# A 64-byte offset for the split weights of 256-column matmuls, and a new order at three places of the even mixer

## Chip, cores and metric

The kernel runs on one core of one Trainium2 chip. The metric is the device time of one execution in microseconds (us), as a median over runs; lower is better. The profiler also takes one execution apart, instruction by instruction; the rows below are from that one.

## The reference

Two layers over 256 latent tokens and 256 context tokens of width 1024. Each layer is: half-step SwiGLU feed-forward, token mixer, half-step SwiGLU feed-forward, each with an RMSNorm that is scaled and shifted by a modulation (made from `c` and `c_ctx`) and a gated residual. Layer 0 mixes with differential attention and a bidirectional mLSTM, layer 1 with gated linear attention; in layer 1 the context stream stops after the mixer's keys and values.

```python
for l in range(DEPTH):
    mx = (s_lat @ ada_w[l] + ada_b[l]).reshape(bsz, N_MOD, 1, d)
    x = x + 0.5 * mx[:, 2] * swiglu(ada_norm(x, norm_g[l, 0], mx[:, 0], mx[:, 1]), ffn_w_in[l, 0], ffn_w_out[l, 0])
    hctx = hctx + 0.5 * mc[2] * swiglu(ada_norm(hctx, ...), ffn_w_in[l, 0], ffn_w_out[l, 0])
    hx = ada_norm(x, norm_g[l, 1], mx[:, 3], mx[:, 4])
    hc = ada_norm(hctx, norm_g[l, 1], mc[3], mc[4])
    yx, yc = even_mixer(...) if l % 2 == 0 else odd_mixer(...)
    x = x + mx[:, 5] * yx
    x = x + 0.5 * mx[:, 8] * swiglu(...)
return rms_norm(x, final_g)
```

## The kernel before

Everything is kept with features on the 128 partitions and tokens on the columns: 8 tiles `xT` of 128x512 (columns 0 to 255 context, `CTX`; 256 to 511 latent, `LAT`). A product in float32 is made of three fp32r matmuls (lines 147 to 150): each operand is split into a high and a low part (`hh`/`hl` or `gh`/`gl` for the activations, `whi`/`wlo` for the weights), and high by high, high by low and low by high are added in PSUM. Each matmul has its own weight load of 128 columns.

Weights come in 1 MB loads (`load`, line 114, on SP's queue) and are split, a tile of 128x1024 at a time, by ScalarE (cast, line 122) and VectorE (subtraction, line 123) into `whi` and `wlo`, two buffers each. Activations `hh`, `hl` are the moving operand with 512 columns (both streams) or 256 (one stream: `CTX` or `LAT`); in `proj_rows` (line 624, the value projections) it is the other way round, the activations are the stationary operand and `whi`, `wlo` move with 256 columns. Where both streams start a stage (`gemm_first`, line 237), the context's columns go first while the latent's norm is still being made; the weights of two of the four tiles there are kept in `wspare`, tiles of the stage's own pool (`split_spare`, line 134).

Where things lie in a partition follows from the order and the size of the tiles in the code, each rounded up to 32 bytes. The pools stand one behind the other: consts (with `unit_e`, 768 bytes, `xT`, `hh`, `hl` of 2048 bytes each), weights (`raw` of 8192, `whi` and `wlo` of 4096), temps, then the pools of the stage. All of these sizes are multiples of 128 from `xT` to `wlo`, except some small ones between `hl` and `raw` that add up to one; so `hh`, `hl`, `gh`, `gl`, `whi` and `wlo` all start at the same place of 128 bytes (64). Two groups stand apart by 64 bytes: `LAST = slice(T - 16, TT - 16)` (line 32) puts the latent activations of the odd mixer's output projection and of the last feed-forward 16 columns (64 bytes) lower, and in the even mixer's pool the two 4-byte tiles `gb` and `gd` (32 bytes each, rounded) push every tile behind them, `wspare` among them, by 64.

The order on each engine is made by a scheduler from the order of the code, the dependences and its own costs; pools with few buffers set when a bank or tile can be taken again. In the even mixer (line 684): `proj_first` makes the mLSTM's q and k, then the gates' product `psg` (24 matmuls, line 752), then the gates' chain on VectorE and ScalarE (lines 763 to 785), four transposes `pmt` of its result (line 788), then head after head, with the value projections (`rows_pair`) and others in between as the scheduler places them. `psg` is in one of the two `mm` banks that `ps_v` and `ps_fm` also use, until line 778 has read it. The two `stack` calls (lines 1013 and 1015) split q and k of the heads for the scores on ScalarE and VectorE. At the mixer's end (lines 1052 to 1063) the last four output tiles are made, `CTX` first, then `LAT` in the order of tiles 2, 3, 0, 1; between the latent tiles the context's norm (one step of factors, eight of `modulate`) is issued in pieces of 0:2, 2:4, 4:6 and the rest. The latent's squares are summed on GpSimd, except those of features 6 and 7, on VectorE (line 260).

Of the kernel before, what the change touches and what calls it, by code (L numbers as in the profile page):

```python
# [17 lines left out]
P = 128  # L18
D = 1024
KC = D // P  # L20
NS = 3
T = 256
# [14 lines left out]
def backbone_kernel(  # L37
# [43 lines left out]
    unit_e = cp.tile([P, 6, 32], F32, name="unit_e")  # L81
    nc.gpsimd.memset(unit_e, 0.0)
    for i in range(6):
        nc.gpsimd.memset(unit_e[:, i, i : i + 1], 1.0)
# [22 lines left out]

    def table(name):
        tc.keep_in_program_order(nc.scalar.preload_act_table_set(name))
# [15 lines left out]
    def split(r3):  # L125
# [3 lines left out]
        hi3 = hi[:, : a * b].rearrange("p (a b) -> p a b", a=a)  # L129
        lo3 = lo[:, : a * b].rearrange("p (a b) -> p a b", a=a)  # L130
        split_into(hi3, lo3, r3)
        return hi3, lo3
# [11 lines left out]
    def half(r3, m):  # L144
        return split(r3[:, :, m * P : m * P + P])
# [39 lines left out]
    def ada_finish(n, acc, pool, ap):  # L185
# [5 lines left out]
        for j in range(4):  # L191
            for i in range(2):
                nc.tensor.matmul(  # L193
                    ps[32 * j : 32 * j + 32, :256],
                    lhsT=unit_e[:, 2 * (n - first) + i],
# [56 lines left out]
    def stat(k, i, sl, apart=False):  # L252
# [43 lines left out]
    def residual(k, ps, gate, i, sl, nxt):  # L296
        residual_at(k, ps[:, sl], gate, i, sl, nxt)

    def residual_at(k, o, gate, i, sl, nxt):
# [3 lines left out]
        stat(k, i, sl, nxt == (1, 2))  # L303

    def out_pass(pairs, streams, units, acts, bank, gate, nxt, between=()):
# [7 lines left out]
        def fetch(mp, k0, nk, ld, m):  # L313
            if m == 0:
                cur["raw"] = ld(mp)
            return half(cur["raw"], m)
# [40 lines left out]
    def ffn_in(l, f, sl, gh, gl, bank, fp, step, j0=0, spare=None, at=None):  # L357
        w_in = ffn_w_in[l, f]
        for j1 in range(j0, NJ, 2):
            js = range(j1, min(j1 + 2, NJ))  # L360
            r = [load(rows(w_in, c0 + j1 * P, len(js) * P)) for c0 in (0, DFF)]
            if spare and j1 == 0:
                ps = [[bank("ps_ab") for _ in range(2)] for _ in js]
                gemm_first(
                    [(ps[0][a], lambda a=a: half(r[a], 0)) for a in range(2)]
# [237 lines left out]
    def proj_fm(w, c0, n, emit, sl=BOTH):  # L603
        for mp in range(n // 2):
            r3 = load(rows(w, c0 + mp * 256, 256))
            for m in range(2):
                wt = half(r3, m)
# [4 lines left out]
    def proj_first(w, c0, emits, bank, sbank, spare):  # L612
# [4 lines left out]
            [(ps[m], lambda m=m: half(r[0], m)) for m in range(2)]  # L617
# [6 lines left out]
    def proj_rows(w, c0, dst, col):  # L624

        r3 = load(rows(w, c0, 256))
        ps = [mm_bank("ps_v") for _ in range(2)]
        for i in range(2):
            wh, wl = split(r3[:, 4 * i : 4 * i + 4])
            for t in range(4):  # L630
                o = ps[t // 2][:, (t % 2) * T : (t % 2) * T + T]
                for k4 in range(4):
# [30 lines left out]
    def out_weights(w, m0, spares):  # L663
# [3 lines left out]
            half(r[t // 2], t % 2) if sp is None else split_spare(r[t // 2], t % 2, sp) for t, sp in enumerate(spares)  # L667
# [16 lines left out]
    def even_mixer(nxt):  # L684
# [54 lines left out]
        graw = mp_.tile([P, KC, 16], F32, name="graw")  # L739
# [11 lines left out]
        psg = mm_bank("psg")  # L751
# [7 lines left out]
        oneh = mp_.tile([P, H2], F32R, name="oneh")  # L759
        for r in (slice(0, H2), slice(H2, P)):  # L760
            nc.vector.tensor_copy(oneh[r], ident[r, r])
# [17 lines left out]
        nc.scalar.copy(gah, ga)  # L779
# [5 lines left out]
        nc.vector.tensor_tensor(mst[H2:P], mst[0:H2], bcum[0:H2], ALU.add)  # L785
        pmt = bank_m("pmt")
        for t in range(4):
            nc.tensor.transpose(pmt[:, t * P : t * P + P], mst[:, t * P : t * P + P], ident)
# [7 lines left out]
        def rows_pair(c0, dst):  # L796
            for i in range(2):
                proj_rows(w_in, c0 + i * T, dst, i * T)
# [5 lines left out]
        def decay_exps(h):  # L804
            E = {}
            for d in range(2):
                pA = bank_m("pA")
                sel = oneh[:, 32 * d + h : 32 * d + h + 1].to_broadcast([P, P])
# [205 lines left out]
        mlstm_head(0, lambda: rows_pair(2048, mv))  # L1014
        mstk.append(stack(mq[1], mq[3], halves2("wTa4", 1) + slots1(("mq0", 1), ("mq2", 1), ("rsa", 1), ("qk3", 1)), (nc.scalar.copy, nc.scalar.copy, nc.scalar.copy, nc.vector, nc.vector)))
# [440 lines left out]
```

## Time and profile before

| what | us |
|---|---|
| median of 3 runs (1784.91 to 1788.17) | 1787.75 |
| the profiled execution's own time | 1790.07 |
| its span, from the first to the last instruction | 1788.4 |
| TensorE busy in the span | 1748.8 (98%) |
| weight loads busy | 1505.4 (84%) |
| VectorE busy | 1151.9 (64%) |
| ScalarE busy | 742.8 (42%) |
| GpSimd busy | 106.7 (6%) |

The profiled execution took 2.3 us more than the median. A matmul's row gives its start and a modelled duration in which it overlaps the next; the pace of a run of matmuls is read from their starts or their number in a stretch, not from the durations.

### The profile page before, as it was taken

How to read it: one execution, taken by the hardware profiler on the slowest of the kernel's cores; microseconds unless marked ns; L12 is line 12 of the kernel's file. 1: busy time of each engine (PE TensorE's matmuls, PEld its weight loads, DVE VectorE, ACT ScalarE, POOL GpSimd, SP SyncE). 2: the span in 40 equal slices, each digit the busy share in tenths (PEclk: the TensorE clock that was granted, in tenths of full speed). 3: DMA queues.
4: the chain of work that ended last, by engine and by line, in shares of the span. 5: the costliest groups of instructions: out<-in, count | busy, mean ns of one | idle time of the engine just before them, and what ended most of it. 6: DMA issues, size and time to landing. Idle time of an engine off the chain costs nothing.

```text
span 1788.4 us, 24901 instructions
## 1 busy us (share of the span) xinstructions
PE 1748.8 (98%) x10087; PEld 1505.4 (84%) x10087; DVE 1151.9 (64%) x1678; ACT 742.8 (42%) x1286; POOL 106.7 (6%) x172
## 2 busy tenths in 40 slices
PE   7999999999999999999999999999999999999998
PEld 5788888899887798888888898888888998889996
DVE  4677776657668866777753485777533737855555
ACT  3422222247558854222222252222322645654443
POOL 1000000003011111000000010000000200010000
PEclk9999999999999999999999999999999999999999
DMA  9555555544121214455543344555442632236553
GB/s 288 189 166 187 188 165 188 171 130 126 48 71 48 95 48 141 165 187 187 188 149 96 126 146 165 188 189 188 143 149 85 190 118 72 80 109 198 187 195 118
DMA packets 209303, 262.30 MB, mean 147 GB/s; under 512 B 6863, under 2 KB 188662, under 8 KB 209188
## 3 DMA queue, kind: packets, MB, share of 16 engines
q1 hardware_dynamic: 208160, 259.28, 44.4%
q8 instruction: 79, 1.29, 0.3%
q0 software_dynamic: 576, 0.84, 0.2%
q10 hardware_dynamic: 452, 0.59, 0.1%
q14 instruction: 36, 0.29, 0.0%
HBM read 259.64 MB, written 1.05 MB: 146 GB/s over the span
## 4 chain that ended last, share of the span: by engine, by line
PE 84%; DVE 8%; ACT 4%; issue 2%; DMA 2%; POOL 0%; SPq 0%; ACTq 0%; POOLq 0%; DVEq 0%
PE ps_ab L148 15%; PE ps_ab L149 15%; PE ps_ab L150 15%; PE ps_y L148 7%; PE ps_y L150 7%; PE ps_y L149 7%; PE ps_fm L150 2%; PE ps_fm L149 2%; PE ps_fm L148 2%; DVE wlo L123 2%; PE po L911 1%; ACT whi L122 1%; PE ada_ps L193 1%; PE ps_l L1386 1%; PE ps_l L1387 1%
## 5 line engine op out<-in xcount | busy, mean ns | idle before, releaser
L122 ACT CAST whi<-raw 128x1024 fp32r<-128x1024 f32 (+1 forms) x326 | 336.3, 1032 | 824.3 <-PE ps_ab L149 451.2
L123 DVE TENSOR_TENSOR wlo<-raw,whi 128x1024 fp32r<-128x1024 f32 (+1 forms) x326 | 392.5, 1204 | 305.9 <-ACT whi L122 301.3
L149 PE MATMUL ps_ab<-hl,whi 128*128 128x512 f32 (+1 forms) x1360 | 483.6, 356 | 2.6 <-POOL hl L279 2.3
L148 PE MATMUL ps_ab<-hh,whi 128*128 128x512 f32 (+1 forms) x1360 | 484.4, 357 | 1.7 <-ACT whi L122 1.0
L150 PE MATMUL ps_ab<-hh,wlo 128*128 128x512 f32 (+1 forms) x1360 | 482.5, 355 | 1.2 <-DVE wlo L123 1.1
L181 DVE SCALAR_TENSOR_TENSOR acc<-raw_ada,cs,acc 128x1024 f32<-128x1024 f32 x224 | 276.5, 1280 | 48.2 <-DMA raw_ada<-in_ada_w_dram 48.1
L148 PEld LDWEIGHTS ps_ab<-hh,whi 128*128 128x128 f32 x1360 | 255.1, 188 | 44.3 <-ACT whi L122 6.6
L149 PEld LDWEIGHTS ps_ab<-hl,whi 128*128 128x128 f32 x1360 | 255.5, 188 | 39.8 <-POOL hl L279 2.9
L150 PEld LDWEIGHTS ps_ab<-hh,wlo 128*128 128x128 f32 x1360 | 255.4, 188 | 38.7 <-DVE wlo L123 1.8
L150 PE MATMUL ps_y<-gh,wlo 128*128 128x512 f32 (+1 forms) x660 | 229.9, 348 | 0.4
L148 PE MATMUL ps_y<-gh,whi 128*128 128x512 f32 (+1 forms) x660 | 230.0, 348 | 0.0
L149 PE MATMUL ps_y<-gl,whi 128*128 128x512 f32 (+1 forms) x660 | 228.8, 347 | 0.0
L150 PEld LDWEIGHTS ps_y<-gh,wlo 128*128 128x128 f32 x660 | 124.9, 189 | 17.6 <-DVE wlo L123 1.5
L148 PEld LDWEIGHTS ps_y<-gh,whi 128*128 128x128 f32 x660 | 124.9, 189 | 17.0 <-ACT whi L122 1.2
L149 PEld LDWEIGHTS ps_y<-gl,whi 128*128 128x128 f32 x660 | 124.9, 189 | 15.5
L353 DVE TENSOR_TENSOR s<-ps_ab,s 128x512 f32<-128x512 f32 (+1 forms) x88 | 54.7, 622 | 118.0 <-PE ps_ab L150 117.9
L260 POOL TENSOR_TENSOR ssum<-ssum,sq 128x256 f32<-128x256 f32 x25 | 26.2, 1049 | 1103.0 <-ACT sq L258 834.4
L148 PE MATMUL ps_fm<-hh,whi 128*128 128x256 f32 (+1 forms) x256 | 83.9, 328 | 0.0
L150 PE MATMUL ps_fm<-hh,wlo 128*128 128x256 f32 (+1 forms) x256 | 83.5, 326 | 0.0
L149 PE MATMUL ps_fm<-hl,whi 128*128 128x256 f32 (+1 forms) x256 | 83.1, 325 | 0.0
L636 PE MATMUL ps_v<-whi,hh 128*128 128x256 f32 x256 | 74.2, 290 | 1.2 <-ACT mv L640 1.2
L637 PE MATMUL ps_v<-wlo,hh 128*128 128x256 f32 x256 | 74.6, 291 | 0.0
(375 smaller groups left out, 2396.3 us busy)
## 6 DMA issues: line engine op xcount, KB each, us to landing
raw<-in_ffn_w_in_dram SPq DMA_DIRECT2D x84, 1024.0 KB, 5.4
raw_ada<-in_ada_w_dram SPq DMA_DIRECT2D x64, 1024.0 KB, 5.0
raw<-in_ffn_w_out_dram SPq DMA_DIRECT2D x41, 1024.0 KB, 4.9
raw<-in_even_w_in_dram SPq DMA_DIRECT2D x12, 1024.0 KB, 5.4
raw<-in_odd_w_in_dram SPq DMA_DIRECT2D x12, 1024.0 KB, 5.5
raw<-in_ffn_w_out_dram SPq DMA_DIRECT2D x15, 768.0 KB, 4.2
raw_c<-in_ada_w_dram SPq DMA_DIRECT2D x16, 512.0 KB, 7.0
raw<-in_even_w_out_dram SPq DMA_DIRECT2D x4, 1024.0 KB, 5.0
```

The costliest lines, as they stand in the source:

```text
L122: nc.scalar.copy(hi3, r3)
L123: eng.tensor_tensor(lo3, r3, hi3.bitcast(F32), ALU.subtract)
L148: nc.tensor.matmul(ps, lhsT=wh, rhs=ah, start=first, stop=False)
L149: nc.tensor.matmul(ps, lhsT=wh, rhs=al, start=False, stop=False)
L150: nc.tensor.matmul(ps, lhsT=wl, rhs=ah, start=False, stop=last)
L181: nc.vector.scalar_tensor_tensor(ada_acc[i], r3[:, k2], s, ada_acc[i], ALU.mult, ALU.add)
L193: nc.tensor.matmul(ps[32 * j : 32 * j + 32, :256], lhsT=unit_e[:, 2 * (n - first) + i], rhs=acc[i][:, j * 256 : j * 256 + 256], start=n == ...
L260: (nc.gpsimd if i and k < KC - 2 else nc.vector).tensor_tensor(ssum[i][0], ssum[i][0], sq, ALU.add)
L353: nc.vector.tensor_tensor(s[:, sl], ps[1][:, sl], s[:, sl], ALU.mult)
L636: nc.tensor.matmul(o, lhsT=ah, rhs=wh[:, k4], start=k == 0 and t % 2 == 0, stop=False)
L637: nc.tensor.matmul(o, lhsT=ah, rhs=wl[:, k4], start=False, stop=False)
L911: nc.tensor.matmul(po[:, t], lhsT=w[:, kt, (t % 2) * P : (t % 2) * P + P], rhs=v[:, kt, h * P : h * P + P], start=kt == 0, stop=kt == nk - 1,)
```

## The change

Three things. First, `split` takes an offset: wherever the moving operand has 256 columns, `whi` and `wlo` are written 16 elements (64 bytes) into their tile, and 48 elements (192 bytes) in `proj_rows`, where they move themselves; with 512 columns it stays 0. The four tiles grow from 4096 to 4352 bytes, and space is found for it: `unit_e` shrinks from 768 to 148 bytes (a window slides over one 1), `oneh` from 256 to 32, `graw` and `lraw` share tiles that are used later. As `unit_e` lies ahead of them, `xT`, `hh`, `hl`, `whi`, `wlo` and the stages' pools start 608 bytes lower: at 96 of 128 bytes instead of 64. Of the 256-column matmuls, 2328 get the offset of 64 bytes between weights and moving columns that they did not have; 288 that read `wspare` in the two feed-forwards and the odd mixer keep offset 0; the 1248 of the last stage keep their 64.

Second, the gates: `psg` moves to a bank of the attention (`bank_a`), the transposes `pmt` are put behind the eighth of the second value projection's groups on TensorE, and the second `stack` is issued after the gates' last ScalarE and VectorE instructions.

Third, the mixer's end: the context's norm is issued in three pieces of three behind the first three latent tiles, and the squares summed on VectorE are those of features 4 and 5, which come last there.

```diff
-    unit_e = cp.tile([P, 6, 32], F32, name="unit_e")
+    unit_e = cp.tile([P, 37], F32, name="unit_e")
...
+    def place(n):
+        return 0 if n == TT else 16
+
+    def split(r3, o=0):
         a, b = r3.shape[1], r3.shape[2]
-        hi = wp.tile([P, 1024], F32R, tag="whi", name="whi", bufs=2)
-        lo = wp.tile([P, 1024], F32R, tag="wlo", name="wlo", bufs=2)
+        hi, lo = (wp.tile([P, WROOM], F32R, tag=t, name=t, bufs=2)[:, o : o + a * b] for t in ("whi", "wlo"))
...
-            wh, wl = split(r3[:, 4 * i : 4 * i + 4])
+            wh, wl = split(r3[:, 4 * i : 4 * i + 4], 64 - place(T))
...
-            (nc.gpsimd if i and k < KC - 2 else nc.vector).tensor_tensor(ssum[i][0], ssum[i][0], sq, ALU.add)
+            (nc.gpsimd if i and k not in late else nc.vector).tensor_tensor(ssum[i][0], ssum[i][0], sq, ALU.add)
...
-        graw = mp_.tile([P, KC, 16], F32, name="graw")
+        graw = mp_.tile([P, TT], F32, tag="qk6", name="graw")[:, : KC * 16].rearrange("p (k n) -> p k n", k=KC)
...
-        psg = mm_bank("psg")
+        psg = bank_a("psg")
...
-        mlstm_head(0, lambda: rows_pair(2048, mv))
-        mstk.append(stack(mq[1], mq[3], ...))
+        values = []
+        mlstm_head(0, lambda: values.extend(rows_pair(2048, mv)))
+        behind(gates_pe, values[1][7])
+        with tc.issue_after(gates_act.ins), tc.issue_after(gates_dve.ins):
+            mstk.append(stack(mq[1], mq[3], ...))
...
-            residual(4 + t, p, gate, *STREAMS[1], nxt)
-            for f in norm[2 * n : 2 * n + 2] if n < 3 else norm[6:]:
+            residual(4 + t, p, gate, *STREAMS[1], nxt, late=(4, 5))
+            for f in norm[3 * n : 3 * n + 3]:
```

On TensorE, the place where the gates' result is transposed (`pmt`), before; 78 rows of `ps_v` stand between the last of `psg` and it:

```order
L638 MATMUL ps_v<-whi,hl_106 128x256
L636 MATMUL ps_v<-whi,hh_99 128x256
L637 MATMUL ps_v<-wlo,hh_99 128x256
L638 MATMUL ps_v<-whi,hl_107 128x256
L788 MATMUL pmt<-ident,t_3490 128x128 x4
L809 MATMUL pA<-gahl,oneh 128x512 x2
L636 MATMUL ps_v<-whi,hh_100 128x256
```

And on TensorE in the changed kernel, with 120 rows of `ps_v` between `psg` and `pmt`:

```order
L654 MATMUL ps_v<-whi,hl_99 128x256
L651 MATMUL ps_v<-whi,hh_92 128x256
L652 MATMUL ps_v<-wlo,hh_92 128x256
L654 MATMUL ps_v<-whi,hl_100 128x256
L809 MATMUL pmt<-ident,t_3487 128x128 x4
L831 MATMUL pA<-gahl,oneh 128x512 x2
L651 MATMUL ps_v<-whi,hh_89 128x256
L879 MATMUL pS<-stk_3516,stk_3515 128x256
```

The transposes have moved 42 matmuls later. On ScalarE, the gates' chain (`t`, `gahl`) before, with the stack's casts (`stk`) between its steps:

```order
L732 ACTIVATE mq_3157<-mq_3157,vec 128x512
L109 ACT_TABLE_LOAD
L848 CAST stk<-mq_3157 64x512
L764 ACTIVATE t_3490<-psg,gb 64x512
L849 CAST stk<-mq_3157 64x512
L765 ACTIVATE t_3490<-t_3490 64x512
L848 CAST stk<-mq_3157 64x512
L766 ACTIVATE t_3490<-t_3490,one_t 64x512
L849 CAST stk<-mq_3157 64x512
L640 COPY mv<-ps_v 128x2x256
L779 CAST gahl<-ga 64x512
L122 CAST whi<-raw 128x1024
```

The same stretch of ScalarE in the changed kernel:

```order
L750 ACTIVATE mq_3152<-mq_3152,vec 128x512
L117 ACT_TABLE_LOAD
L785 ACTIVATE t_3487<-psg,gb 64x512
L786 ACTIVATE t_3487<-t_3487 64x512
L787 ACTIVATE t_3487<-t_3487,one_t 64x512
L130 CAST whi<-raw 128x1024
L800 CAST gahl<-ga 64x512
L869 CAST stk_3878<-mq_3150 64x512
L870 CAST stk<-mq_3152 64x512
L871 CAST stk<-mq_3152 64x512
L657 COPY mv<-ps_v 128x2x256
```

The casts now stand behind the chain. On VectorE, the end of the mixer before: `xT_90` and `xT_91` are the residuals of the last two latent tiles, `u` of 92 and 93 the context's last two norm steps:

```order
L260 TENSOR_TENSOR ssum<-ssum,sq 128x256
L300 SCALAR_TENSOR_TENSOR xT_90<-ps_y,md,xT_90 128x256
L282 SCALAR_TENSOR_TENSOR hl_106<-u,md,hh_98 128x256
L123 TENSOR_TENSOR wlo<-raw,whi 128x1024
L273 SCALAR_TENSOR_TENSOR u<-xT_92,amp,rstd 128x256
L273 SCALAR_TENSOR_TENSOR u<-xT_93,amp,rstd 128x256
L300 SCALAR_TENSOR_TENSOR xT_91<-ps_y,md,xT_91 128x256
L282 SCALAR_TENSOR_TENSOR hl_108<-u,md,hh_100 128x256
L123 TENSOR_TENSOR wspare<-raw,wspare 128x512 x4
```

The same in the changed kernel, where the numbers are 5 lower (`u` of 87 and 88 are the last two norm steps):

```order
L131 TENSOR_TENSOR wlo<-raw,whi 128x1024
L296 SCALAR_TENSOR_TENSOR hl_101<-u,md,hh_93 128x256
L314 SCALAR_TENSOR_TENSOR xT_85<-ps_y,md,xT_85 128x256
L287 SCALAR_TENSOR_TENSOR u<-xT_87,amp,rstd 128x256
L287 SCALAR_TENSOR_TENSOR u<-xT_88,amp,rstd 128x256
L274 TENSOR_TENSOR ssum<-ssum,sq 128x256
L296 SCALAR_TENSOR_TENSOR hl_103<-u,md,hh_95 128x256
L314 SCALAR_TENSOR_TENSOR xT_86<-ps_y,md,xT_86 128x256
L131 TENSOR_TENSOR wspare<-raw,wspare 128x512
L274 TENSOR_TENSOR ssum<-ssum,sq 128x256
L131 TENSOR_TENSOR wspare<-raw,wspare 128x512 x3
```

The weights' subtraction (`wlo`) has moved ahead of the residual, and two sums of squares have come to VectorE from GpSimd.

## Rows read from the trace of the kernel before

**Rows 1.** Page, part 1: busy us, share, instructions of each engine.

```profile
PE 1748.8 (98%) x10087; PEld 1505.4 (84%) x10087; DVE 1151.9 (64%) x1678; ACT 742.8 (42%) x1286; POOL 106.7 (6%) x172
```

**Rows 2.** Groups by form, TensorE: line, tiles, shapes, count | busy us, mean ns | idle.

```profile
L148 PE MATMUL ps_ab<-hh,whi 128*128 128x512 f32 x944 | 368.9, 391 | 0.0
...
L148 PE MATMUL ps_ab<-hh,whi 128*128 128x256 f32 x416 | 115.6, 280 | 1.7 <-ACT whi L122 1.0 <-ACT hh L278 0.4 <-ACT hh L281 0.2
...
L636 PE MATMUL ps_v<-whi,hh 128*128 128x256 f32 x256 | 74.2, 290 | 1.2 <-ACT mv L640 1.2
```

**Rows 3.** Windows, TensorE: stretch, us, busy (matmuls), granted clock, DMA.

```profile
1049.50:1069.30 19.80, 19.80 (x167) 1.00 0.47 160
...
1640.00:1677.00 37.00, 37.00 (x329) 1.00 0.63 204
...
1205.00:1215.00 10.00, 10.00 (x46) 1.00 0.44 147
```

**Rows 4.** Timeline, TensorE, even mixer's first projection: start, us, instruction.

```profile
416.61 0.28 PE L148 MATMUL ps_fm<-hh,wspare 128*128 128x256 f32 x1
...
422.27 0.28 PE L148 MATMUL ps_fm<-hh,whi 128*128 128x256 f32 x1
...
428.02 0.28 PE L148 MATMUL ps_fm<-hh,wspare 128*128 128x256 f32 x1
...
433.68 0.40 PE L148 MATMUL psg<-hh,stk 128*128 128x512 f32 x1
...
439.28 0.28 PE L636 MATMUL ps_v<-whi,hh 128*128 128x256 f32 x1
```

**Rows 5.** Timeline, TensorE, gates: the two waits.

```profile
446.41 0.39 PE L636 MATMUL ps_v<-whi,hh 128*128 128x256 f32 x1 [1.23 <-ACT mv L640]
...
453.52 1.12 PE L788 MATMUL pmt<-ident,t 128*128 128x128 f32 x4 [3.26 <-DVE t L785]
```

**Rows 6.** Timeline, ScalarE and VectorE: the gates' chain.

```profile
441.08 0.62 ACT L848 CAST stk<-mq 64x512 fp32r<-64x512 f32 x1
...
444.38 0.72 ACT L766 ACTIVATE t<-t,one_t 64x512 f32<-64x512 f32 x1
...
445.14 0.68 DVE L767 TENSOR_TENSOR t<-t,t 64x512 f32<-64x512 f32 x1
...
452.78 0.68 DVE L785 TENSOR_TENSOR t<-t,t 64x512 f32<-64x512 f32 x1
```

**Rows 7.** Windows and timeline, TensorE, behind the gates' wait: clock and pace.

```profile
455.00:460.00 5.00, 5.00 (x26) 0.54 0.00 0
460.00:465.00 5.00, 5.00 (x42) 1.00 0.01 3
...
456.36 0.41 PE L638 MATMUL ps_v<-whi,hl 128*128 128x256 f32 x1
456.57 0.41 PE L636 MATMUL ps_v<-whi,hh 128*128 128x256 f32 x1
...
466.30 0.44 PE L898 MATMUL pt<-ident,E 128*128 128x128 f32 x2 [0.34 <-DVE E L886]
```

**Rows 8.** Timeline, the mixer's end: TensorE's waits, then GpSimd.

```profile
672.71 0.38 PE L148 MATMUL ps_ab<-hh,whi 128*128 128x256 f32 x1 [0.17 <-ACT hh L281]
673.35 0.39 PE L149 MATMUL ps_ab<-hl,whi 128*128 128x256 f32 x1 [0.26 <-DVE hl L282]
...
674.28 0.38 PE L148 MATMUL ps_ab<-hh,whi 128*128 128x256 f32 x1 [0.43 <-ACT hh L278]
676.12 0.39 PE L149 MATMUL ps_ab<-hl,whi 128*128 128x256 f32 x1 [1.45 <-POOL hl L279]
...
674.08 0.85 POOL L260 TENSOR_TENSOR ssum<-ssum,sq 128x256 f32<-128x256 f32 x1 [2.25 <-ACT sq L258]
674.89 1.17 POOL L279 TENSOR_TENSOR hl<-u,hh 128x256 fp32r<-128x256 f32 x1
```

**Rows 9.** Windows, all engines, the odd mixer's value projections: busy us of each.

```profile
1475.00:1560.00 85.00, 80.73 (x587) 73.63 (x586) 69.95 (x142) 51.27 (x108) 7.65 (x24) 1.00 0.22 71
```

More of the change, by code (lines that the diff above doesn't have):

```diff
@@ L21 @@
 NS = 3
+WROOM = 1024 + 64
 T = 256
@@ L80, in backbone_kernel @@
     nc.vector.tensor_reduce(sel4, ident.rearrange("p (j r) -> p r j", j=4)[:, 0:2], AX.X, ALU.add)
-    unit_e = cp.tile([P, 6, 32], F32, name="unit_e")
+    unit_e = cp.tile([P, 37], F32, name="unit_e")
     nc.gpsimd.memset(unit_e, 0.0)
-    for i in range(6):
-        nc.gpsimd.memset(unit_e[:, i, i : i + 1], 1.0)
+    nc.gpsimd.memset(unit_e[:, 5:6], 1.0)
     eps_t = cp.tile([P, 1], F32, name="eps_t")
@@ L106, in backbone_kernel, with behind @@
     g_gla = vec[:, 77:79]
+    def behind(ins, first):
+        tc.add_manual_dep(
+            ins.ins, first.ins.name,
+            mybir.DependencyInfo(mybir.DependencyClass.NoSync, mybir.DependencyReason.DATA), reason="order",
+        )
     def table(name):
@@ L142, in rows, with half, width @@
         return w[k0 * P : (k0 + nk) * P, c0 : c0 + n].rearrange("(k p) n -> p k n", p=P)
-    def half(r3, m):
-        return split(r3[:, :, m * P : m * P + P])
+    def half(r3, m, o=0):
+        return split(r3[:, :, m * P : m * P + P], o)
+    def width(sl):
+        return sl.stop - sl.start
     def mm3(ps, wh, wl, ah, al, first, last):
@@ L194, in ada_finish @@
                     ps[32 * j : 32 * j + 32, :256],
-                    lhsT=unit_e[:, 2 * (n - first) + i],
+                    lhsT=unit_e[:, 5 - 2 * (n - first) - i : 37 - 2 * (n - first) - i],
                     rhs=acc[i][:, j * 256 : j * 256 + 256],
@@ L250, in gemm_first, with stat @@
             gemm_h(t[0], w, LAT)
-    def stat(k, i, sl, apart=False):
+    def stat(k, i, sl, apart=False, late=(KC - 2, KC - 1)):
         if k == 0:
@@ L315, in fetch @@
                 cur["raw"] = ld(mp)
-            return half(cur["raw"], m)
+            return half(cur["raw"], m, place(width(sl)))
         w = fetch(*halves[0])
@@ L364, in ffn_in @@
                 gemm_first(
-                    [(ps[0][a], lambda a=a: half(r[a], 0)) for a in range(2)]
+                    [(ps[0][a], lambda a=a: half(r[a], 0, place(T))) for a in range(2)]
                     + [(ps[1][a], lambda a=a: split_spare(r[a], 1, spare)) for a in range(2)],
@@ L606, in proj_fm @@
             for m in range(2):
-                wt = half(r3, m)
+                wt = half(r3, m, place(width(sl)))
                 ps = mm_bank("ps_fm")
@@ L616, in proj_first @@
         gemm_first(
-            [(ps[m], lambda m=m: half(r[0], m)) for m in range(2)]
+            [(ps[m], lambda m=m: half(r[0], m, place(T))) for m in range(2)]
             + [(ps[2 + m], lambda m=m: split_spare(r[1], m, spare)) for m in range(2)],
@@ L758, in even_mixer @@
         gah, gal = gahl[0:H2], gahl[H2:P]
-        oneh = mp_.tile([P, H2], F32R, name="oneh")
-        for r in (slice(0, H2), slice(H2, P)):
-            nc.vector.tensor_copy(oneh[r], ident[r, r])
+        oneh = mp_.tile([P, 8], F32R, name="oneh")
+        for r in (0, H2):
+            for d in range(2):
+                nc.vector.tensor_copy(
+                    oneh[r : r + H2, 4 * d : 4 * d + 4], ident[r : r + H2, r + 32 * d : r + 32 * d + 4]
+                )
         t0, t1, t2 = t2k("dg", "t0", 2), t2k("dg", "t1", 2), t2k("rsm", "t2")
@@ L796, in rows_pair @@
         def rows_pair(c0, dst):
-            for i in range(2):
-                proj_rows(w_in, c0 + i * T, dst, i * T)
+            return [proj_rows(w_in, c0 + i * T, dst, i * T) for i in range(2)]
         def keys(t):
@@ L1051, in even_mixer @@
                 residual(t, ps[t], gate, *st, nxt)
-        ws = out_weights(w_out, 4, (new, new, None, None))
+        ws = out_weights(w_out, 4, (new, new, None, None), place(T))
         ps = [b("ps_y") for b in (bank_a, bank_a, bank_a, bank_m)]
```

38 lines of the change are left out of this document (21 added, 17 removed).

## Prediction

> **What bounds the kernel now.** I first read the page's share of each engine: TensorE is busy 1748.8 of 1788.4 us (98%), VectorE 64%, ScalarE 42% [rows 1]. With so little idle time a change pays on TensorE alone, in two ways: its matmuls follow one another faster, or its few waits go. So the next view is the pace. In the groups by form a matmul of 256 columns has a modelled duration of 280 to 290 ns and one of 512 of 391 ns [rows 2]; these overlap, so I count starts instead. In a stretch of feed-forward with one stream, 167 matmuls are in progress within 19.80 us; the first and last stick out by about 2.3 places (0.28 us over 0.12), so the pace is 19.8 / 164.7 = 120.2 ns. In the last feed-forward the same count gives 37.00 / 326.7 = 113.3 ns [rows 3]. The clock is 1.00 in both; operands, shapes and products are of one kind. By the layout described above, the first stretch has weights and moving columns at the same place of 128 bytes, the second 64 bytes apart.
>
> The timeline of the even mixer's first projection shows the same within 23 us [rows 4]. The starts of the four blocks lie at 416.61, 422.27, 428.02, 433.68: 48 matmuls on `wspare` (64 apart) in 5.66 us = 117.9 ns, 48 on `whi`/`wlo` (0 apart) in 5.75 us = 119.8, 48 on `wspare` again in 5.66. Then `psg`, 24 matmuls of 512 columns with weights from that pool, also 64 apart, in 5.60 us = 233.3 ns; the ordinary ones with 512 columns and distance 0 go at 10.00 / 44.3 = 226 ns [rows 3]. So the distance counts, in opposite directions for 256 and 512 columns, which is just what the change sorts by. But two paces stand for "64 apart, 256 columns", 113.3 and 117.9. In the slower the weights start at 0 of 128 and the moving columns at 64; in the faster it is the reverse.
>
> **The offset (A).** Of the 2328 matmuls that get it, 1560 have activations moving with 256 columns (264 in each of three feed-forwards, ffn00, ffn01 and ffn10, 288 in the even mixer's projections, 96 + 96 + 288 in the first projections elsewhere), 768 are `ps_v`, 384 in each mixer. The gain of one is 120.0 − 113.3 = 6.7 ns if they reach the last stage's pace, 2.1 ns if only that of `wspare`. In the changed layout the weights lie at 32 and the moving columns at 96, a pair that no row shows; I take the faster value, since it is that of 1248 matmuls and the slower of only 96, and since with the slower pair the weights sit at the start of the 128 bytes, which nothing does afterwards. 1560 × 6.7 = 10.4, of which I book 10, as some of them wait for a norm or a cast anyway. For `ps_v` the full price is 768 × 6.7 = 5.1 us. In the odd mixer they stand in a stretch where VectorE is busy 69.95 of 85 us and TensorE idles 4.3 [rows 9], so part of a faster pace turns into waiting for the splits: I take 3.5. A = 13.5 us; bounds 0 and 15.5.
>
> The offsets cost the splitting engines nothing that I can see: `whi` and `wlo` have the same shapes, only their start moves by whole 32-byte steps. No row shows a cast to such a place, so a few ns per cast either way stay open; ScalarE at 42% hides them. The 4617 matmuls of 512 columns keep distance 0, but at 96 of 128 instead of 64; I take 0 and come back to it as a rival. The smaller `unit_e`, the shared tags of `graw` and `lraw` and the shorter `oneh` change memsets and two loads that are needed long after their issue; I book nothing, and 0.5 us either way.
>
> **The gates (B).** TensorE waits twice [rows 5]: 1.23 us at 446.41 behind a copy of ScalarE (`mv`, out of a bank of the pool that `psg` blocks), and 3.26 us at 453.52, where the transposes `pmt` wait for VectorE's last `t`. With `psg` in another bank the first has no reason left. For the second, two things move. On ScalarE three casts of `stk` of 0.62 us [rows 6], 1.9 us together, leave the stretch between `psg` and the chain. On TensorE 120 `ps_v` instead of 78 stand before `pmt`: 42 × 0.12 = 5.0 us more cover against a wait of 3.3. VectorE gets a `wlo` into this stretch (about 1.2 us), which the removed casts pay for. Both waits go: 4.5 us.
>
> Behind the wait the granted clock is 0.54 in the stretch 455 to 460, that is, mostly the lower of the two levels, after the engine had stood for 3.26 us; the `ps_v` are 0.21 us apart, and 26 of them are in progress against 42 in the next 5 us [rows 7]. 16 × 0.12 = 1.9 us are lost there, and the short `pmt` and `pA` before it run slow too, for which I estimate 0.7 from the 1.12 us that the transposes' row lasts. If the wait goes, this 2.6 us goes.
>
> What is late next: the first head's `pt` waits 0.34 us for `E` [rows 7], 12.8 us behind `pmt`. The chain from `pmt` to `E` goes over ScalarE and VectorE and keeps its length, while TensorE's filler between them falls from 64 to 60 `ps_v`, runs at full clock now and at the faster pace, and the casts of `stk` and a copy of `mv` stand on ScalarE right behind the chain. Filler then lasts 60 × 0.114 = 6.8 us plus `pA` and the scores, some 9.5 to 11 in all against a chain that I put at 10.3 to 12.8; I take a new wait of 1.5 us. B = 4.5 + 2.6 − 1.5 = 5.6; I book 5.5; bounds 1 and 8.
>
> **The mixer's end (C).** Between 672.7 and 676.2 four waits add up to 0.17 + 0.26 + 0.43 + 1.45 = 2.31 us of idle time [rows 8]; each of the stalled matmuls also starts a pipeline anew, so that by starts some 3 us are lost. The largest is for the last `hl`, which GpSimd makes in 1.17 us after a `ssum` of 0.85 that came in late behind ScalarE's square. In the new order that square's sum is on VectorE, and the last norm step is about 1.1 us earlier, since one residual now comes after it rather than before. The last `hl` should come about 2 us earlier. I leave 1 us of the 3 as a remaining stall: C = 2; bounds −1 and 3.
>
> **Sum.** 13.5 + 5.5 + 2.0 = 21.0 us from the profiled execution's 1790.07, giving 1769.1. That execution took 2.3 us more than the median; against the median it is 1787.75 − 21 = 1766.8, or 1767.
>
> **Rivals.**
>
> *The offset does nothing (R1).* For it: the fast and the slow pace of [rows 3] stand in different stages, so that something else of the stage could make them differ. Against it, [rows 4] alternate within one stage, on one set of moving columns, 117.9, 119.8, 117.9. A = 0 gives 1767 + 13.5 = 1780. The Trainium skill ("TensorE: Matmul & The Clock Gate", section "Step-by-step: what each phase is for") says that TensorE has two independent SBUF read ports, so that loading the next weights takes nothing from the running matmul. By that rule the distance could not matter; the alternation in this trace disagrees with it by 1.9 ns of 119.8, and the last stage by 6.7. Chance 0.08.
>
> *The absolute place counts too (R2).* Then the pair 32 and 96 may have the 117.9 ns of `wspare`: A = 1560 × 2.1 + 3.5 = 6.8 and 1773. `ps_v` has the reverse pair (weights at 96, moving at 32), so either could be the slow one. If also the 1248 of the last stage, which move from the fast pair to (32, 96), fell to 117.9, that costs 1248 × 4.6 = 5.7: 1779. Chance 0.20, mostly for the first.
>
> *The 608 bytes cost the wide matmuls (R3), the slower side.* 4617 matmuls of 512 columns keep their distance, but every operand moves by 32 bytes within its 128. If a start at an odd multiple of 32 costs them what 64 apart costs `psg`, 233.3 − 226 = 7.3 ns, they lose 33.7 us: 1767 + 33.7 = 1801. It decides from 21.0 / 4617 = 4.5 ns each. For it: [rows 4] show that the wide form reacts to layout. [...] Chance 0.08.
>
> *The waits come back (R4).* The first head's chain bounds the gates, so that the 4.5 us reappear at `pt`, and at the mixer's end VectorE, with two more sums, holds the residuals back: B + C = 0, 1774. For it: VectorE is in every one of these chains and gets work in both places. Against it: no wait on VectorE of more than 3.3 us is in the rows, and the clock's 1.9 us would come back in any case if TensorE is no longer idle for long. Chance 0.10.
>
> **How the numbers follow.** The main case keeps 0.54; its own range is 1762 to 1772 (A between 11 and 15.5, B + C between 4 and 10, the profile's 2.3 us either way at half weight). R2 and R4 lie at 1773 to 1779, R1 at 1780 and, joined with a small R4, up to 1784: 1760 to 1784 leaves out R3 and a little at either end, about 0.2. A measurement of this kernel can tell about 0.2%, 3.6 us, from no change. Faster by more than that are the main case, R2, R4, and nearly all of R1: 0.87. Slower: R3 from its deciding point on, 0.08. The remaining 0.05 are mixtures of R1 with R4, or R3 at about 4 ns.
>
> **What would show it.** In the changed profile, a one-stream stretch of ffn00 should have a pace of 113.3 ns (R2: 117.9; R1: 120.0), `ps_v` in the even mixer likewise, and wide stretches still 226 to 227 (R3: 233). At the gates no wait at `pmt` and a granted clock of 1.00 throughout; a wait of 1 to 2 us at the first `pt`, over 4 if R4 holds. At the mixer's end at most one wait of about 1 us for the last `hl`. I am wrong if the paces have not changed where the distance has, if wide matmuls have slowed, or if the two places in the even mixer lose under a third of the 10 us that they cost now.

## The result and the profile after

The changed kernel takes 1774.91 us (median of 4 runs, 1772.0 to 1776.99) against 1786.33 us for the kernel before (4 runs in the same comparison): ratio 0.9933, 95% interval 0.9918 to 0.9948. It is faster by 11.4 us, where 21 was forecast as the likeliest and 1760 to 1784 as the range. The profiled execution is the one of 1776.99 us.

TensorE's line of the page, beside [rows 1], has the same instructions and 11 us less busy time:

```profile
PE 1737.9 (98%) x10087; PEld 1497.0 (84%) x10087; DVE 1148.7 (65%) x1680; ACT 743.0 (42%) x1286; POOL 106.9 (6%) x167
```

The pace, in windows of TensorE in the changed kernel (stretch, us and busy, number of matmuls, granted clock, DMA share, GB/s):

```profile
376.00:388.00 12.00, 12.00 (x104) 1.00 0.53 176
1002.00:1014.00 12.00, 12.00 (x105) 1.00 0.56 176
1435.00:1448.00 13.00, 13.00 (x117) 1.00 0.56 167
1600.00:1637.00 37.00, 37.00 (x316) 1.00 0.59 190
1668.00:1705.00 37.00, 37.00 (x329) 1.00 0.59 198
1115.00:1125.00 10.00, 10.00 (x46) 1.00 0.63 211
```

Counted as in [rows 3], less 2.3: the output of ffn00 goes at 12.00 / 101.7 = 118.0 ns, that of ffn01 at 12.00 / 102.7 = 116.8 (117.8 in both, from start to start), the odd mixer's projections at 13.00 / 114.7 = 113.3. The last stage is the surprise. Its offset did not change, and it had 113.3 throughout before; now the stretch 1600 to 1637 has 37.00 / 313.7 = 117.9 and 1668 to 1705 has 113.3. These are two paces in one stage of one execution, on the same kind of matmul, both with the weights at 96 of 128 bytes and the moving columns at 32. The wide matmuls are as before (46 in 10 us).

At the gates, TensorE's timeline of the changed kernel (start, us, instruction, idle time before it):

```profile
449.67 0.60 PE L809 MATMUL pmt<-ident,t 128*128 128x128 f32 x4
450.03 0.70 PE L831 MATMUL pA<-gahl,oneh 128*128 128x512 f32 x2
450.57 0.28 PE L651 MATMUL ps_v<-whi,hh 128*128 128x256 f32 x1
453.12 0.36 PE L879 MATMUL pS<-stk,stk 128*128 128x256 f32 x1 [2.27 <-DVE em L816]
```

VectorE in the same stretch:

```profile
448.08 0.68 DVE L806 TENSOR_TENSOR t<-t,t 64x512 f32<-64x512 f32 x1
448.69 0.68 DVE L872 TENSOR_TENSOR stk<-mq,stk 64x512 fp32r<-64x512 f32 x1
...
451.54 1.23 DVE L131 TENSOR_TENSOR wlo<-raw,whi 128x1024 fp32r<-128x1024 f32 x1
452.69 0.18 DVE L815 TENSOR_SCALAR negm<-pmt 128x32 f32<-128x32 f32 x1
```

And the clock there:

```profile
450.00:455.00 5.00, 2.73 (x16) 0.84 0.20 39
455.00:460.00 5.00, 5.00 (x35) 0.82 0.51 174
```

Both waits of [rows 5] are gone: `pmt` starts with no idle time. A new one of 2.27 us (2.55 between starts) stands 3.5 us behind `pmt`, at the first head's scores `pS`. VectorE's reading of `pmt` (`negm`, `em`) had come behind four `stk` subtractions of 0.68 us, which had moved there with the held stack, and a `wlo` of 1.23. Behind that wait the clock falls to its lower level for a part, as it did before.

At the mixer's end the waits in TensorE's timeline of the changed kernel, for [rows 8]:

```profile
662.42 0.39 PE L163 MATMUL ps_ab<-hl,whi 128*128 128x256 f32 x1 [0.20 <-DVE hl L296]
663.54 0.39 PE L163 MATMUL ps_ab<-hl,whi 128*128 128x256 f32 x1 [0.42 <-POOL hl L293]
664.42 0.70 PE L305 MATMUL ms<-ssum,ones_d 128*128 128x256 f32 x2 [0.38 <-DVE ssum L274]
```

1.00 us in place of 2.31; GpSimd makes the last `hl` from 662.75 in 0.73 us, with no `ssum` ahead of it.

Stage by stage, from the first matmul of a kind to the first of the next, in six profiled executions (us; e1, e2, e5 and e8 are experiments below; "even mixer" begins at its first `ps_v`):

| stage | before | before again (e5) | changed | e1, no offset | e2, old orders | e8 |
|---|---|---|---|---|---|---|
| start to ffn00's output | 283.20 | 277.47 | 280.63 | 280.95 | 280.10 | 277.44 |
| ffn00 output of 256 columns, even projections | 62.53 | 62.55 | 61.91 | 62.50 | 61.91 | 61.18 |
| even mixer | 230.93 | 229.76 | 223.81 | 222.94 | 228.67 | 222.30 |
| ffn01's first projection | 26.82 | 28.35 | 25.09 | 25.16 | 28.27 | 25.09 |
| ffn01 output of 256 columns | 34.04 | 34.03 | 33.69 | 34.03 | 33.69 | 33.69 |
| ffn10's first projection | 23.54 | 23.52 | 23.24 | 23.52 | 23.25 | 23.25 |
| ffn10 output of 256 columns, odd projections | 95.57 | 95.58 | 93.54 | 95.57 | 93.52 | 93.79 |
| odd mixer's `ps_v` | 83.88 | 83.86 | 83.78 | 83.91 | 83.78 | 83.75 |
| last feed-forward | 125.44 | 125.83 | 127.33 | 128.17 | 128.35 | 126.25 |

The stages of 512 columns differ by 0.1 us at most. So the orders brought most of it (even mixer and the border behind it), the offset some 3 us in small pieces, and three rows vary with the execution: the start, ffn01's first projection (by the clock, see e7) and the last feed-forward.

### The profile page after: what moved, and what is told of

Its sections match the earlier page's. It is cut to its first block, busy times and chain, and to the rows that moved or that the text cites. A ratio compares the mean times of both kernels' runs of the same rounds, so it can differ in the third digit from the quotient of the medians.

```text
span 1775.3 us, 24902 instructions
## 1 busy us (share of the span) xinstructions
PE 1737.9 (98%) x10087; PEld 1497.0 (84%) x10087; DVE 1148.7 (65%) x1680; ACT 743.0 (42%) x1286; POOL 106.9 (6%) x167
## 4 chain that ended last, share of the span: by engine, by line
PE 85%; DVE 8%; ACT 4%; issue 2%; DMA 1%; POOL 0%; SPq 0%; ACTq 0%; POOLq 0%; DVEq 0%
PE ps_ab L162 16%; PE ps_ab L163 16%; PE ps_ab L164 16%; PE ps_y L162 7%; PE ps_y L164 7%; PE ps_y L163 7%; PE ps_fm L164 2%; PE ps_fm L162 2%; PE ps_fm L163 2%; DVE wlo L131 2%; PE po L933 1%; ACT whi L130 1%; PE ada_ps L207 1%; PE ps_l L1413 1%; PE ps_l L1414 1%
```

## Experiments

Each is an edit of the changed kernel, but for e5. Times are medians; the ratios are against the kernel before, run beside it. Two theories of the pace stand against each other in e3, e4, e9 (P: the place within 128 bytes picks it; S: it settles anew where a stretch begins).

**e1: all offsets 0.**

```diff
-        return 0 if n == TT else 16
+        return 0
-            wh, wl = split(r3[:, 4 * i : 4 * i + 4], 64 - place(T))
+            wh, wl = split(r3[:, 4 * i : 4 * i + 4], 0)
```

> The changed kernel with every offset set to 0 (same order on every engine, same 96 of 128 for the tiles; the last stage keeps its 64). Theory 1 (offset and orders both pay, about half each): the 256-column paces of the earlier stages go back to 120.0 ns, some 1780 to 1781 us. Rival (the orders paid for all of it, the offset nothing): 1775, paces apart from that as in the changed kernel. Rival (the orders gave back what they took): 1785.

Measured: 1775.83 us, ratio 0.9948 (0.9932 to 0.9964). This comes out with the rival: the orders pay for nearly all of it. But the paces did go back (TensorE's windows in e1):

```profile
376.00:388.00 12.00, 12.00 (x102) 1.00 0.53 176
1600.00:1637.00 37.00, 37.00 (x316) 1.00 0.52 171
1668.00:1705.00 37.00, 37.00 (x316) 1.00 0.51 171
```

102 instead of 104 in the first: 120 ns. So the offset does change the pace, and hardly the time. One stage explains a part of that: the even mixer is 0.9 us shorter than in the changed kernel, since `pS` waits 1.51 us instead of 2.27 and the clock stays up. The last feed-forward, with its distance of 64, was at 117.9 all through here, which made e1's profiled execution longer, not shorter (128.17 us against 127.33). That execution took 1780.63 us, 4.8 above e1's median, so the stages are compared below without the start and the last feed-forward.

```profile
454.03 0.35 PE L879 MATMUL pS<-stk,stk 128*128 128x256 f32 x1 [1.51 <-DVE em L816]
```

```profile
450.00:455.00 5.00, 3.49 (x28) 1.00 0.02 5
455.00:460.00 5.00, 5.00 (x42) 1.00 0.64 208
```

**e2: the orders of before, with the offset.**

```diff
-        psg = bank_a("psg")
+        psg = mm_bank("psg")
-        behind(gates_pe, values[1][7])
-        with tc.issue_after(gates_act.ins), tc.issue_after(gates_dve.ins):
-            residual(4 + t, p, gate, *STREAMS[1], nxt, late=(4, 5))
-            for f in norm[3 * n : 3 * n + 3]:
+            residual(4 + t, p, gate, *STREAMS[1], nxt)
+            for f in norm[2 * n : 2 * n + 2] if n < 3 else norm[6:]:
```

> The changed kernel with the orders of the gates and of the mixer's end put back as before. Theory 1: the gates' two waits (1.2 and 3.3 us), the half clock behind them and the wait of 1.8 us at the mixer's end are back, 1781 us. Rival (the offset alone pays): 1775. Also: stretches ahead of the gates (the output of the first feed-forward, 133 and 72 matmuls at 117.8 ns, 20 and 16 between them at 114) have an unchanged program; if the pace at a distance of 64 bytes is a matter of chance per execution, they come out differently here, if it is fixed by the program, the same.

Measured: 1784.00 us over 12 runs, ratio 0.9988 (0.9977 to 0.9999). That is above the 1781 expected. The offset alone is worth about 2 us; both orders beside it 9.1 (1784.0 to 1774.9). In ffn00's output the same instructions show nearly the same paces as in the changed kernel (133 and 72 matmuls at 117.8, 20 between them at 114); one stretch of 17 at 402 us went at 117.8 where the changed kernel has 113.9.

**e3 and e4: the tiles at 0 and at 64 of 128 bytes.** The edit of e3; in e4 the number is 61.

```diff
-    unit_e = cp.tile([P, 37], F32, name="unit_e")
+    unit_e = cp.tile([P, 45], F32, name="unit_e")
```

> The changed kernel with 8 more columns in unit_e, so that hh, hl, whi, wlo start at 0 of 128 bytes; order and distances the same. Two paces, 113.4 and 117.8 ns, stand for distance 64 in the changed kernel, at one and the same place. Theory P (the place picks the pace, as in the kernel before, where weights at 64 and moving at 0 had 113.4 and the reverse 117.8): all non-ps_v offset stretches (weights 64, moving 0) at 113.4, ps_v and the last stage (weights 0, moving 64) at 117.8; 1773 to 1775 us. Theory S (the pace is settled anew at each restart after a wait, whatever the place): both paces in each of these groups; 1772 to 1778.

> As the run before, with 24 more columns in unit_e: tiles at 64 of 128 bytes, as in the kernel before. Theory P: the non-ps_v offset stretches (weights 0, moving 64) at 117.8 ns, ps_v and the last stage (weights 64, moving 0) at 113.4; 1771 to 1774 us. Theory S: both paces in each group; 1772 to 1778.

Measured: 1775.41 us, ratio 0.9939 (0.9923 to 0.9955), and 1774.12 us, 0.9923 (0.9908 to 0.9939). Theory P falls. In e3 ffn00's output has weights at 64 and moving columns at 0, the pair of the last stage of before with its 113.4, and goes at 118 ns; its last stage, with the reverse pair, has 260 matmuls at 113.4 and then 741 at 117.8. TensorE's windows of e3:

```profile
376.00:388.00 12.00, 12.00 (x104) 1.00 0.54 176
1630.00:1645.00 15.00, 15.00 (x130) 1.00 0.49 165
```

and of e4, where ffn00's output has the reverse pair and the same pace:

```profile
376.00:388.00 12.00, 12.00 (x104) 1.00 0.54 176
1630.00:1645.00 15.00, 15.00 (x135) 1.00 0.43 142
```

**e5: the kernel before, unchanged.**

> The kernel before, unchanged, for a second look. All five kernels with the changed layout reach the output of the first feed-forward at 373.6 to 374.5 us of their span, the kernel before at 376.7. Theory: those 2.3 to 3.1 us are chance of one execution (the clock in the first 30 us), and this look shows about 374. Rival: the smaller unit_e brings them, and this look shows 376 to 377 again.

Measured: 1785.09 us, one execution. It reaches ffn00's output at 371.0 us, earlier than any of the changed layout until then. The 5.7 us between two executions of one program arise in the first 31 us, and 3.3 of them from 18 us on, where the clock is granted at its lower level in one of the two. In the kernel before:

```profile
24.00:26.00 2.00, 2.00 (x8) 0.50 1.22 290
26.00:30.00 4.00, 4.00 (x12) 0.56 1.12 339
```

In e5:

```profile
24.00:26.00 2.00, 2.00 (x16) 1.00 1.23 294
26.00:30.00 4.00, 4.00 (x35) 1.00 1.10 342
```

The other 2.4 us had arisen by 18 us. There the same matmuls follow one another at about half the rate in the kernel before (first line) as in e5 (second), though the clock's column reads 1.00 in both; that it was the clock there too is a guess.

```profile
14.13 1.97 PE L503 MATMUL px<-ident,xs 128*128 128x128 f32 x8
13.58 1.09 PE L503 MATMUL px<-ident,xs 128*128 128x128 f32 x8
```

So no gain of the change is shown in the start. The last feed-forward of e5 was at 113.4 throughout, as in the profile of before.

**e6: the gates' order of before** (`psg`, `behind` and `issue_after` as in e2).

> The changed kernel with the gates' order of before (psg in its mm bank, pmt and the second stack in the order of the code); offset and the mixer's end as changed. Theory: the waits of 1.5 and 3.4 us at mv and pmt and the half clock are back, the wait of 2.3 us at pS goes: 5 us of the 9 that both orders brought beside the offset, 1779 to 1781 us. Rival (the gates' order only moves the wait to pS and gains nothing): 1775.

Measured: 1779.42 us, ratio 0.9955 (0.9944 to 0.9967). The gates' order is worth 4.5 us beside the offset. The intervals of the two ratios overlap a little, but the stage shows it: the even mixer takes 228.69 us against 223.81, and TensorE's idle time in it is 11.78 us against 6.85. The waits of before are back in TensorE's timeline of e6:

```profile
442.43 0.39 PE L651 MATMUL ps_v<-whi,hh 128*128 128x256 f32 x1 [1.51 <-ACT mv L657]
449.54 1.11 PE L809 MATMUL pmt<-ident,t 128*128 128x128 f32 x4 [3.43 <-DVE t L806]
460.86 0.44 PE L920 MATMUL pt<-ident,E 128*128 128x128 f32 x2 [0.41 <-DVE E L908]
```

Behind `pmt` the clock is lower by about as much as behind `pS` in the changed kernel (0.84 and 0.82 there):

```profile
445.00:450.00 5.00, 1.57 (x12) 0.92 0.00 0
450.00:455.00 5.00, 5.00 (x33) 0.74 0.00 0
```

Its last stage, at the addresses and with the instructions of the changed kernel, was at 113.4 from 1593 to 1708. This speaks for chance.

**e7: the mixer's end of before** (the last four lines of e2's edit).

> The changed kernel with the mixer's end of before; offset and gates as changed. Theory: the wait for the last hl is back, 1.8 us between two starts, in all 3 us more at the border: 1777 to 1778 us. Rival (the end's order is worth nothing, the norm being late anyway): 1775.

Measured: 1777.52 us, ratio 0.9947 (0.9934 to 0.9960). The end's order is worth 2.6 us by the medians. The intervals of the two ratios overlap, but the stage shows it: ffn01's first projection takes 28.03 us against 25.09. Its wait in TensorE's timeline of e7, and the clock behind it:

```profile
665.90 0.58 PE L163 MATMUL ps_ab<-hl,whi 128*128 128x256 f32 x1 [1.44 <-POOL hl L293]
665.00:669.00 4.00, 3.10 (x13) 0.57 0.66 209
```

Some 1.5 us of these 2.9 are the clock and not the wait. The same wait of 1.45 us stands in both executions of the kernel before; behind it the clock stays up in the first (first line) and falls in e5 (second), and the stage takes 26.82 and 28.35 us.

```profile
676.00:680.00 4.00, 3.88 (x31) 1.00 0.81 279
669.50:673.50 4.00, 4.00 (x21) 0.57 0.99 318
```

With the old end the clock fell there in three traces of four (e2, e5, e7), with the new one in one of ten (e3, 26.81 us). Where it fell in neither, from the first profile of before to the changed kernel, the stage lost 1.73 us.

**e8: another entry, and the even mixer's `ps_v` at distance 0.**

```diff
+            return half(cur["raw"], m, place(width(sl)) if o is None else o)
-                w = fetch(*halves[n + 1])
+                w = fetch(*halves[n + 1], o=16 if n + 2 == len(halves) else None)
...
-            return [proj_rows(w_in, c0 + i * T, dst, i * T) for i in range(2)]
+            return [proj_rows(w_in, c0 + i * T, dst, i * T, 0) for i in range(2)]
```

> Two edits of the changed kernel, order unchanged. First, the last weights of the 512-column pass ahead of the three 256-column passes (ffn00, ffn01, ffn10) get the offset too. Theory S (the pace at distance 64 is set where a stretch is entered and then kept: 15 of 15 entries at once from the pace of 120 or 227 ns, distance 0, gave 117.8; 6 of 7 from that of 233 gave 113.4): the 133 matmuls there, at 117.8 ns in all of five runs, go at 113.4, for 24 at 233 instead of 227 each, net 0.4 us each. Rival (the pace belongs to the place in the program or the buffers): 117.8 as before. Second, ps_v in the even mixer at distance 0. Theory (the faster filler only came to the wait for the stack sooner and slowed the clock behind it): the wait of 2.3 us at pS falls to about 1.6, the clock stays at 1.00, and the stretch from the first ps_v to ffn01 is 0.8 us shorter, not 1.7 longer. In all 1772 to 1774 us.

Measured: 1772.00 us, ratio 0.9919 (0.9907 to 0.9931). The first part missed: the 133 matmuls went at 117.8 in all three places, though the matmuls ahead of them now went at 233 ns. TensorE's timeline and window there in e8:

```profile
370.60 0.40 PE L163 MATMUL ps_y<-gl,whi 128*128 128x512 f32 x1
370.84 0.39 PE L164 MATMUL ps_y<-gh,wlo 128*128 128x512 f32 x1
371.07 0.28 PE L162 MATMUL ps_y<-gh,whi 128*128 128x256 f32 x1
```

```profile
372.00:384.00 12.00, 12.00 (x104) 1.00 0.53 176
```

So what stood ahead does not pick the pace by its own distance. The second part held: the wait at `pS` is 1.50 us, the clock is 1.00, the even mixer takes 222.30 us, 1.5 less than in the changed kernel.

**e9: tiles at 64 of 128 bytes, the even mixer's `ps_v` at distance 0** (e4's edit and the second of e8).

> Tiles at 64 of 128 bytes as in e4, and ps_v of the even mixer at distance 0 as in e8. Theory: what e8 gained came from that ps_v; the wait at pS is 1.8 us between starts again and the clock stays up: 1771 to 1773 us. On the last stage: at (weights 64, moving 0) all its stretches had 113.4 ns in three executions of three, at (96, 32) in one of six. Theory P2 (that place favours the fast pace): all at 113.4 again. Theory S (chance after each wait): some stretch at 117.8 in this or the next run.

Measured: 1772.99 us, ratio 0.9918 (0.9903 to 0.9932). The even mixer takes 222.37 us, as in e8. Of the last feed-forward's matmuls 635 went at 113.4 and 400 at 117.8, at the very place where three executions had shown 113.4 alone: P2 falls too.

**e10: tiles at 64 of 128 bytes, every offset 0** (the edits of e4 and e1).

> Tiles at 64 of 128 bytes, every offset 0: the orders of the change and nothing else beside sizes. Theory: the offset is worth little here, since its gain in the feed-forwards (2.2 to 6.6 ns for 1560 matmuls) meets a loss in the even mixer; 1774 to 1777 us, within 2 us of e4 (1774.1). Rival (e1 was near the changed kernel only because its last stage fell to 117.8 ns in the profiled execution): with the last stage at 113.4 the time is 1771 to 1773, and the offset is a loss.

Measured: 1776.27 us, ratio 0.9945 (0.9930 to 0.9959). 2.1 us above e4, its twin with the offset; the intervals of the ratios overlap. The rival (the offset is a loss, once the last stage goes at 113.4) could not be read from the time, as the last stage of the profiled execution went mostly at 117.8 (777 of 1051). The stages settle it: without the start, the last feed-forward and the stages of 512 columns they add up to 547.6 us in e10 against 545.4 in e4, and to 547.6 in e1 against 545.1 in the changed kernel. So the offset is a gain of 2.2 to 2.6 us there, whatever the last stage does.

**e11: the second stack not held back.**

```diff
-        with tc.issue_after(gates_act.ins), tc.issue_after(gates_dve.ins):
-            mstk.append(stack(mq[1], mq[3], ...))
+        mstk.append(stack(mq[1], mq[3], ...))
```

> The changed kernel without holding the second stack back behind the gates' chain (bank of psg and place of pmt as changed; order of TensorE the same). Theory: the chain ends 2 us later, at pmt a wait of 1 to 1.5 us comes, and the wait at pS (2.3 us, behind stack and wlo on VectorE) shrinks by as much: 1774 to 1776 us. Rival (holding it back is what the gain of the gates rests on): 1778 or more.

Measured: 1773.87 us, ratio 0.9930 (0.9919 to 0.9942). TensorE's waits in e11:

```profile
446.95 0.38 PE L651 MATMUL ps_v<-whi,hh 128*128 128x256 f32 x1 [0.51 <-ACT mv L657]
450.95 0.66 PE L809 MATMUL pmt<-ident,t 128*128 128x128 f32 x4 [0.99 <-DVE t L806]
453.09 0.35 PE L879 MATMUL pS<-stk,stk 128*128 128x256 f32 x1 [0.90 <-DVE em L816]
```

2.40 us of idle time in three pieces instead of 2.27 in one; the clock stays at 1.00, and the even mixer takes 222.88 us, 0.9 less. Holding the stack back is not what the gates' gain rests on.

**e12: `psg` back in its old bank** (`mm_bank("psg")`).

> The changed kernel with psg back in a bank of the pool of ps_v and ps_fm; place of pmt and held stack as changed. Theory: the wait for mv (1.5 to 1.8 us between starts) is back ahead of pmt, and as the chain ends no later, a part of it shows: 1775.5 to 1777 us. Rival (the 42 matmuls more ahead of pmt cover it all): 1775.

Measured: 1775.14 us, ratio 0.9938 (0.9923 to 0.9954), not told apart from the changed kernel. In its trace the wait is back, and the clock falls behind it (0.89 from 440 to 445 us, 0.77 from 445 to 450):

```profile
443.46 0.36 PE L651 MATMUL ps_v<-whi,hh 128*128 128x256 f32 x1 [1.84 <-DVE ga L799]
```

The wait at `pS` is gone in turn, and the even mixer takes 224.74 us, 0.9 more. With the held stack (e11) and the bank (e12) each undone at little cost, the place of `pmt` is what is left to carry most of the gates' gain. That is argued, not shown: it wasn't tried alone.

## Why the prediction was right in sign and short in size

The forecast (faster, clear of noise, inside its range) held; the sum of 21 was made of terms that failed and held as follows.

- **The offset (A), booked at 13.5, brought 1 to 4.** This is the step that failed: "I take the faster value, since it is that of 1248 matmuls and the slower of only 96". The medians give 0.9 (e1 to the changed kernel) and 2.1 (e10 to e4), the ratios to the kernel before 2.7 and 3.9; the stage table, changed against e1, gives 0.59 + 0.34 + 0.28 + 2.03 + 0.13 = 3.4 us in five stages, less 0.9 in the even mixer. Three things took the rest.
  - *The pace.* At distance 64 a stretch goes at 113.4 or at 117.8 ns. In the changed kernel, of the matmuls that got the offset and the even mixer's `wspare` that had it (without the last stage), about 870 went at the faster and about 1500 at the slower. The slower is worth 2.1 ns, not 6.7. Both paces were in [rows 4] and [rows 3]; I took them for a matter of place (R2), and chose between them by counting matmuls where I should have counted stretches: 1248 matmuls were few stretches, all of one kind. R4's 1774 and R2's 1773 are the nearest numbers of all, but by luck: e6 and e7 refute the reason of R4, and e3, e4 and e9 that of R2.
  - *The waits for weights.* The prediction let 0.4 of 10.4 us go for them, which was too little. In ffn10's output (264 matmuls of 256 columns) the intervals of more than 126 ns between starts add up to 2.02 us before and to 2.73 in the changed kernel. From its first start to its last such a pass takes 32.48 to 32.52 us in all twelve cases at distance 0 (three feed-forwards in four traces), and 32.06 to 32.19 in all thirty at distance 64, though the paces in it differ. In the changed kernel 73 matmuls in its middle went at 117.8 in ffn00 and at 113.5 in ffn10. The next one started 0.42 us behind them in ffn00 (first line) and 0.70 in ffn10 (second), there behind VectorE's `wlo` (third), and the pass took 32.07 us in both. So the faster pace turned into waiting there:

```profile
402.08 0.39 PE L164 MATMUL ps_y<-gh,wlo 128*128 128x256 f32 x1
1399.12 0.39 PE L164 MATMUL ps_y<-gh,wlo 128*128 128x256 f32 x1 [0.42 <-DVE wlo L131]
1398.12 0.94 DVE L131 TENSOR_TENSOR wlo<-raw,whi 128x768 fp32r<-128x768 f32 x1
```

  - *`ps_v`, booked at 3.5.* In the odd mixer 0.1 us came of it, in the even mixer less than nothing. There they are the filler behind which the gates' chain runs; when the filler is faster, the wait behind it is longer (1.51 to 2.27 us, e1 against the changed kernel), and the clock falls on top. Bringing them back to distance 0 (e8, e9) shortens the even mixer by 1.5 us.
- **The gates (B), booked at 5.5,** measured 4.5 (e6 to the changed kernel) and 4.9 us in the stage. The two waits went as forecast, but that the size came out is in part luck. The new wait of 1.5 us was foreseen at the first `pt`, and came as 2.27 us at `pS`, from VectorE's late reading of `pmt`. I had counted the moved `stk` casts on ScalarE and not their subtractions on VectorE. The half clock that was to go, 2.6 us of the sum, came back with it and is as long in the changed kernel as in e6. Without the offset the stage lost more, 230.3 (mean of two executions) to 222.9 us; there the wait at `pS` is 1.51 us and the clock stays at 1.00. What made up for the wait and the clock is above all another wait that went, and that the sum did not have. It stands in all four traces with the old gates (before, e2, e5, e6) and is at most 0.35 us in the others; in the kernel before it is 1.86 us between starts:

```profile
506.29 0.66 PE L920 MATMUL pt_o<-ident,on 128*128 128x128 f32 x4 [1.47 <-DVE on L917]
```

- **The mixer's end (C), booked at 2.0,** measured 2.6 (e7) and 2.9 us in the stage. The mechanism is the one that was named, the last `hl` on GpSimd behind a late sum, and by itself it is worth 1.7 us. The rest is a clock that falls behind that wait in some executions (e7), which the sum did not have.
- **The wide matmuls** kept their pace: R3 is refuted by 46 in 10 us at 96 of 128, and by stages equal to 0.1 us.
- **R1** (the offset does nothing) is wrong in mechanism, as the paces changed just where the distance did; but its A of 0 is nearer to what was measured than the 13.5. The Trainium skill ("TensorE: Matmul & The Clock Gate", "Step-by-step: what each phase is for") has it that loading the next weights takes no read bandwidth from the running matmul. The runs do not agree with what R1 made of that: e1 shows, as the trace of before did, 120 ns at distance 0 against 113.4 or 117.8 at 64, with only the offset changed. **R4** (the mixer's waits come back) came true for a part, at `pS`, and not for the whole.
- **The profiled execution's own time.** I took its 2.3 us above the median for a level shift. e5 shows that its start alone was 5.7 us slower than in another execution.
- **Slips of counting.** Of the 1560 matmuls 192 are in the even mixer and 384 in the odd mixer's projections, not 288 and 288; the total holds. The last stage moved to weights at 96 and moving columns at 32, the pair of `ps_v`, and not the reverse as R2 has it. The trace has 4908 matmuls of 512 columns, and which of them make up the 4617 of R3 is not clear; as their pace did not change, nothing hangs on it.

What stays open is what picks the pace at distance 64. Over the fourteen traces, stretches of ten or more that follow at once on matmuls at distance 0 (paces 120 or 227 ns) had 117.8 in all of some 80 cases. All others, mostly behind a wait, had 113.4 in some 340 cases and 117.8 in some 220 (the counts shift a little with where a stretch is taken to begin), and the last stage differed between kernels that have the same instructions and addresses there (the changed kernel, e2, e6, e7). It isn't the place (e3, e4, e9), and not the distance of the matmuls ahead (e8). How load and matmul stand to one another at the restart would be a guess.

## What to carry to other kernels

Read a pace from several stretches, and count stretches that began apart, not matmuls: a long stretch is one sample of whatever was settled at its start. Before pricing faster filler, ask what it fills; in front of a wait its gain turns into waiting, and a longer wait can cost the clock too. Before booking a faster pace, find what else bounds the stage: here a stretch of 73 matmuls at the faster pace did not shorten its pass, as the weights behind it came no sooner. When work is moved behind a chain, follow every instruction of it on every engine, up to the first reader of the chain's result.

## What the runs showed of the hardware

- The pace of these matmuls depends on the distance of the next weights from the moving columns in 128 bytes: 256 columns, 120.0 ns at 0 and 113.4 or 117.8 at 64; 512 columns, 226.8 at 0 and 233.3 at 64. The place of both together does not matter (tiles at 0, 64 and 96 of 128).
- At distance 64 one of two paces holds until the next wait. The last feed-forward alone took 124.2 to 128.4 us by that, 4 us between traces of like code. Beside the start (277.4 to 283.2 us up to ffn00's output) no other stage spreads as much among traces of like code.
- The first 31 us differed by 5.7 us between two executions of one program, 3.3 of them from 18 us on, where the clock was granted at its lower level in one (e5).
- A wait of 1.51 us at `pS` left the granted clock at 1.00 (e1), 2.27 us at the same place brought stretches of 0.84 and 0.82 behind it; three waits that add up to 2.40 us (e11) left it at 1.00.
- The same wait does not always cost the clock: one of 1.45 us at the mixer's end left it at 1.00 in one execution of the kernel before and was followed by 0.57 in the other (e5).
